# Two projections as seven block products: a hybrid streaming encoder step on one core

## The chip, the core and the metric

The kernel runs on one core of a Trainium2 chip. The metric is device time in microseconds (us) of one execution; lower is better. TensorE (PE) multiplies matrices into the eight banks of PSUM; VectorE (DVE), ScalarE (ACT) and GpSimd (POOL) do elementwise work; SyncE (SP) issues the DMA transfers between DRAM and SBUF. Before the change three runs took 1732.12, 1733.9 and 1737.66 us, median 1733.9. A difference under 0.3% (5 us) cannot be told from none.

## What is computed

One layer over 4096 prompt tokens and 32 sample tokens, width 1024, all in float32:

```
h = rmsnorm_pre(x); z = h @ w_in        # 1024 -> 2832 columns
aq 512, ak 128, av 128, ag 512, gq 256, gk 256, gv 512, gg 512, glr 16 = split(z)
attn = window_attention(rotary(aq), rotary(ak), av, sinks) * silu(ag)   # 8 heads, own chunk of 64 and the 2 before
log_a = log_sigmoid(glr @ w_gk_up + b_gk) / 16
o, state = gla_chunked(gq, gk, gv, log_a, s0)                           # 4 heads, recurrent state
o = rmsnorm(o) * silu(gg)
y = x + rmsnorm_post(concat(attn, o) @ w_out)
```

Outputs are y for prompt and sample, the last K and V rows, and the new states.

## The kernel before

**Arithmetic.** A float32 operand is split into two fp32r parts, high and low (`split` L111, `split_w` L115). A product is three matmul passes: x_high·w_high, x_high·w_low, x_low·w_high. The 32 sample tokens are stacked as high rows and low rows of one stationary tile, so that two passes do, and the two row groups are added afterwards.

**Blocks and stages.** The tokens go in 16 blocks of 256, two tiles of 128. Three stages follow one another, each over all blocks. (1) GLA: q and k are projected transposed (columns of w_in as the stationary operand, 256 tokens as the moving one: `proj_T2`, L188), then values, gates and the low-rank column group for each token tile with x as the stationary operand and 384 + 384 + 272 weight columns moving (`proj_N`, L202). A chain of small matmuls per block (decay, scores, state, output, L437 to L533) runs beside the projections of the next block; its result goes to `mixg_d` in DRAM. (2) Attention: five pairs of column tiles per block (k and v; two pairs of gates; two pairs of q), all by `proj_T2`. The chain per token tile: V transposed (L718), scores (L753), maximum, exponentials (L773), sum and scaling (L783), probabilities transposed (L800), values (L816, L824), times the gate; result to `mixa_d`. (3) Output projection: 512 + 512 columns per token tile with x as the stationary operand, then the norm and the residual (L896 to L904). Stage 2 and stage 1 both load x again from DRAM and split it (ScalarE the high part, GpSimd the low part, L112 and L113).

**Rotation.** q and k leave PSUM by ScalarE (raw, L628). VectorE shuffles (sw, L629), GpSimd multiplies by the sine rows (L630), VectorE multiplies raw by the cosine rows (L631) and adds both (L633).

**What sets the order.** TensorE's order is written out by a program. The projection of a block is a generator that yields after some matmuls and says how long these take; each chain is a generator that says after how much of that time its next step is due. A chain of block b is put into its lane when the projection of b is through, and between two parts of the projection every chain step that is due is issued. In the attention chain the wait after the scores is 9800 (in ns of such time) and after the transposes 2700. The last GLA block's chain waits 17000, so that the lane lags behind during the whole of stage 2. The order on the other engines comes from a scheduler.

**Memory.** Working tiles have rings of their own (`BUFS`, six classes); weights have slots wa, wb, wc that are loaded anew for each stage.

## Time and profile before

| | |
|---|---|
| median of three runs | 1733.9 us |
| the profiled execution | 1728.69 us, its span 1726.9 us |
| first matmul | 6.41 us |
| stages | GLA to about 690 us, attention to about 1317, output to 1718.5, then the last norm and store |
| mean granted TensorE clock | 0.992 |

The span goes from the first to the last instruction. A granted clock of 1 is 2.4 GHz, 0.5 is 1.2 GHz.

### The profile page before, as it was taken

To read this page: it belongs to the slowest core of one execution; us is meant where nothing else is said; L and a number is where in the kernel's file an instruction comes from. 1 tells how busy PE (TensorE), PEld (TensorE's weight loads), DVE (VectorE), ACT (ScalarE), POOL (GpSimd) and SP (SyncE) were. 2 spreads that over 40 slices of the span, in tenths; PEclk is the share of its full clock that TensorE was granted. 3 is DMA by queue.
4 is the path that set the end of the run, shared out by engine and by line. 5 is a ranking of instruction groups with operands and counts; after the bars stand their busy time and mean duration, and the time that the engine had idled before them with its cause. 6 is when DMAs were issued, how large, how long until landed. Compare 5 with 4: busy or idle time off the path is not lost. (4 is left out here: it accounts for less than half of the span.)

```text
span 1726.9 us, 31972 instructions
## 1 busy us (share of the span) xinstructions
PE 1680.6 (97%) x12584; PEld 1549.0 (90%) x12584; DVE 875.1 (51%) x2201; ACT 717.2 (42%) x1902; POOL 467.6 (27%) x425
## 2 busy tenths in 40 slices
PE   8899999999999999999999999999999899999998
PEld 8799999999999999999999889999998688888886
DVE  5444444454444445755555556455557633343333
ACT  7444444444444444534344344454445422222221
POOL 3222222221222222343333333333432122212220
PEclk9999999999999999999999999999999999999999
DMA  8322222221212222521111112111214444444441
GB/s 278 44 65 65 65 65 68 69 64 59 70 65 65 65 65 83 132 57 58 54 55 48 49 47 62 48 48 47 64 42 142 143 129 141 143 122 147 146 137 65
DMA packets 130855, 146.01 MB, mean 85 GB/s; under 512 B 27936, under 2 KB 103792, under 8 KB 130704
## 3 DMA queue, kind: packets, MB, share of 16 engines
q1 hardware_dynamic: 130704, 143.96, 28.1%
q8 instruction: 99, 1.62, 0.4%
q14 instruction: 52, 0.43, 0.1%
HBM read 109.67 MB, written 34.26 MB: 83 GB/s over the span
## 5 line engine op out<-in xcount | busy, mean ns | idle before, releaser
L113 POOL TENSOR_TENSOR oxl<-xst,oxh 128x512 fp32r<-128x512 f32 x64 | 82.7, 1295 | 286.1 <-DMA xo<-in_x 113.9
L773 ACT ACTIVATE pp<-pss,nb 128x192 f32<-128x192 f32 (+3 forms) x260 | 105.2, 426 | 90.1 <-DVE nb L759 66.1
L113 POOL TENSOR_TENSOR gxl<-xst,gxh 128x512 fp32r<-128x512 f32 (+1 forms) x63 | 82.2, 1307 | 167.3 <-ACT gxh L112 101.0
L896 DVE TENSOR_TENSOR yw<-pso,npw 128x512 f32<-128x512 f32 x64 | 44.2, 692 | 160.7 <-PE pso L202 160.1
L897 ACT ACTIVATE yt<-pso 128x512 f32<-128x512 f32 x64 | 38.1, 595 | 181.3 <-DVE yw L896 181.3
L424 POOL TENSOR_TENSOR xg<-xg,esg 128x512 f32<-128x512 f32 (+1 forms) x33 | 42.9, 1299 | 254.4 <-ACT esg L423 248.8
L113 POOL TENSOR_TENSOR axl<-xst,axh 128x512 fp32r<-128x512 f32 (+1 forms) x64 | 87.5, 1380 | 66.7 <-ACT axh L112 47.4
L630 POOL TENSOR_TENSOR sw<-sw,rows 128x512 f32<-128x512 f32 (+1 forms) x50 | 66.4, 1328 | 104.6 <-DVE sw L629 97.7
L672 POOL TENSOR_TENSOR sgT<-sgT,ea 128x512 f32<-128x512 f32 (+1 forms) x34 | 41.9, 1234 | 184.8 <-ACT ea L671 183.2
L783 DVE TENSOR_SCALAR pp<-pp,ll 128x192 f32<-128x192 f32 (+3 forms) x260 | 83.3, 395 | 1.1
L755 DVE TENSOR_REDUCE mx<-pss 128x2 f32<-128x384 f32 (+3 forms) x130 | 63.4, 542 | 26.9 <-PE pss L753 26.8
L202 PE MATMUL psn<-gch,gxh 128*128 128x272 f32 x256 | 73.7, 288 | 0.0
L202 PE MATMUL psn<-gcl,gxh 128*128 128x272 f32 x256 | 73.6, 287 | 0.0
L202 PE MATMUL psn<-gch,gxl 128*128 128x272 f32 x256 | 73.5, 287 | 0.0
L112 ACT ACTIVATE oxh<-xst 128x512 fp32r<-128x512 f32 x64 | 40.3, 630 | 53.2 <-DMA xst<-mixa_d 20.7
L518 ACT ACTIVATE og<-po 128x256 f32<-128x256 f32 (+1 forms) x66 | 21.7, 381 | 93.3 <-PE po L515 93.3
L485 DVE COPY_PREDICATED ats<-msk,pa 128x256 f32<-128x256 uint8 (+1 forms) x66 | 25.3, 436 | 67.1 <-PE pa L483 67.1
L112 ACT ACTIVATE axh<-xst 128x512 fp32r<-128x512 f32 (+1 forms) x64 | 40.9, 644 | 41.8 <-PE psa L188 25.8
L773 ACT ACTIVATION_READ_ACCUMULATOR pp<-pss,nb 128x1 f32 x260 | 55.9, 215 | 0.0
L633 DVE TENSOR_TENSOR q<-raw,sw 128x512 f32<-128x512 f32 (+1 forms) x34 | 39.2, 1153 | 30.3 <-POOL sw L630 30.3
L800 PE MATMUL ppT<-ident,pp 128*128 128x128 f32 (+1 forms) x388 | 49.3, 275 | 4.5 <-DVE vT L650 4.0
L804 ACT COPY pT<-ppT 128x512 f32<-128x512 f32 (+1 forms) x65 | 35.1, 585 | 44.2 <-PE ppT L800 44.1
(872 smaller groups left out, 6036.4 us busy)
## 6 DMA issues: line engine op xcount, KB each, us to landing
xst<-in_xT SPq DMA_DIRECT2D x128, 256.0 KB, 2.8
xn<-in_x SPq DMA_DIRECT2D x32, 512.0 KB, 5.2
xo<-in_x SPq DMA_DIRECT2D x64, 256.0 KB, 3.8
out_y<-yt SPq DMA_DIRECT2D x64, 256.0 KB, 2.5
wst<-in_w_in SPq DMA_DIRECT2D x32, 256.0 KB, 5.1
mixg_d<-mxg SPq DMA_DIRECT2D x16, 512.0 KB, 4.2
mixa_d<-sgT SPq DMA_DIRECT2D x16, 512.0 KB, 2.9
xst<-mixa_d SPq DMA_DIRECT2D x32, 256.0 KB, 2.7
```

The costliest lines, as they stand in the source:

```text
L112: nc.scalar.activation(hi, src, AF.Copy)
L113: (eng or nc.vector).tensor_tensor(lo, src, hi.bitcast(F32), op=ALU.subtract)
L202: nc.tensor.matmul(pss[g], a, w_of(k_, hl, g), start=(k_ == 0 and i == 0), stop=(k_ == KC - 1 and i == len(passes) - 1))
L424: nc.gpsimd.tensor_tensor(xg, xg, e, op=ALU.mult)
L630: nc.gpsimd.tensor_tensor(sw, sw, c["RS"].unsqueeze(1).to_broadcast([P, m, n]), op=ALU.mult)
L633: nc.vector.tensor_tensor(out, rv, sv, op=ALU.add)
L672: nc.gpsimd.tensor_tensor(xa, xa, e, op=ALU.mult)
L755: nc.vector.tensor_reduce(mx[:, u, g], pss[u, g][:, :, :nk], axis=AX.X, op=ALU.max)
L773: nc.scalar.activation(pps[g][b][:, u, o_ : o_ + nk], pss[u, g][:, b, :nk], AF.Exp, scale=0.125, bias=nb[:, u, g, b : b + 1], accum_out=ll ...
L783: nc.vector.tensor_scalar(pv, pv, ll[:, u, g, b : b + 1], None, op0=ALU.mult)
L800: nc.tensor.transpose(ps[:rows, g, b], src, ident)
L896: nc.vector.tensor_tensor(yw[g], pss[g][:pt], O["npw"][:pt, 512 * g : 512 * g + 512], op=ALU.mult)
```

## The change

**Products.** Two projections are computed block-wise, by the seven products of Strassen's method in Winograd's form: values/gates (2 × 260 columns for either half of the columns; 512 values or gates and 8 of the 16 low-rank columns make 520) and the output projection (2 × 512). One unit is a pair of token tiles × the two halves of K × the two halves of the columns. From the quarters A11, A12, A21, A22 of x come the sums T1 to T4, from the quarters of the weights V11, V12, V21, V22 the sums S1 to S4; seven products instead of eight are accumulated in the banks Y, X and Z, and each result is put together at the exit of a bank. Block 0 does without: it has 192 matmuls of 260 columns (output: 96 of 512) on V11, S1 = V22 + V21, V22 and V12. The sample rows take 64 (output: 32). Blocks 1 to 15 have 168 (output: 84). The weights S2, S3, S4 are made during block 0. For block b the products are issued as `stage_b` of b, `stage_a` of b+1, `stage_c` of b.

**Four stages.** (1) values/gates go to DRAM (`vl_d`, `gl_d`), silu applied to the gates; (2) q, k and the attention gates, 192 matmuls of 256 columns per block, with the GLA chain; x's split parts and the attention gates go to DRAM (`xs_d`, `sg_d`); (3) k, v, q of attention, 144 matmuls per block, with the attention chain, x read already split; (4) output. A chain may now be launched in the middle of a projection (`launch`). The attention chain waits 7400 after the scores and 100 after the transposes, and the values of a tile follow two tiles later. Half of the scaling of the probabilities moves to ScalarE.

**Slots.** Working tiles share slots with the weights (`RINGS`: per stage a list of slots in turn).

```diff
-    BUFS = {"A": (2048, 6), "B": (2048, 6), "C": (2048, 6), "D": (2048, 7), "E": (4096, 3), "F": (1024, 9)}
+    COMBOS = ("V11", "V12", "S1", "S2", "S3", "V22", "S4")
+    RINGS = {
+        "raw1": k_(*range(6)), "T1": k_(6, 7, 8, 9), "out1": k_(*range(10, 17)), "e1": k_(17, 18),
...
+        "rs": k_(0, 1, 2, 3), "rows": k_(12, 13), "kb": k_(14, 15, 18), "vT": k_(4, 5), "q": k_(*range(6, 12)),
...
+    def product(outs, name, x_, first):
+        xh, xl = x_
+        n = outs[0].shape[1]
+        for j, o_ in enumerate(outs):
+            for k in range(4):
+                wh, wl = [t_[:, j * n : j * n + n] for t_ in W[name][k]]
+                for i, (a, b) in enumerate(((xh, wh), (xh, wl), (xl, wh))):
+                    nc.tensor.matmul(o_, a[:, k], b, start=(first and k == 0 and i == 0), stop=(k == 3 and i == 2), skip_group_check=True)
+            yield 12 * n / 2.4, j
...
+    def stage_a(c, ng, n, ev):
+        c["Y"] = [mm_bank("psY")[:, :n] for _ in range(ng)]
+        for t_, j in product(c["Y"], "V11", c["A11"], True):
+            ev(c, "P1", j)
+            yield t_
+        c["X"] = [ch_bank("psX")[:, :n] for _ in range(ng)]
+        for t_, j in product(c["X"], "V12", c["A12"], True):
...
+    def stage_b(c, ng, n, ev):
+        for t_, j in product(c["Y"], "S2", c["T2"], False):
+            ev(c, "P6", j)
+            yield t_
+        c["Z"] = [ch_bank("psZ")[:, :n] for _ in range(ng)]
+        for t_, j in product(c["Z"], "S3", c["T3"], True):
+            yield t_
+        for t_, j in product(c["Y"], "S1", c["T1"], False):
...
+    def stage_c(c, ng, n, ev):
+        for t_, j in product(c["Y"], "S4", c["A22"], False):
...
+        for t_, j in product(c["Z"], "V22", c["T4"], False):
...
+        def s34(k, with_s2):
+            st, s1, v11 = s2(k)
+            if with_s2:
+                split(*w_combo("S2", k, n), st, nc.gpsimd)
+            nc.vector.scalar_tensor_tensor(s1, s1, sc(1, k), v11, op0=ALU.mult, op1=ALU.subtract)
+            s3h, s3l = w_combo("S3", k, n)
+            nc.scalar.activation(s3h, s1, AF.Copy, scale=-1.0)
+            nc.vector.scalar_tensor_tensor(s3l, s1, -1.0, s3h.bitcast(F32), op0=ALU.mult, op1=ALU.subtract)
+            v12 = ld(1, 2, k)
+            nc.vector.scalar_tensor_tensor(v12, v12, sc(2, k), st, op0=ALU.mult, op1=ALU.subtract)
+            split(*w_combo("S4", k, n), v12, nc.gpsimd)
...
-        pairs = [gs[:2], gs[2:], kvs, qs[:2], qs[2:]] if blk == 0 else [kvs, gs[:2], gs[2:], qs[:2], qs[2:]]
-        for pair in pairs:
+        for pair in (kvs, qs[:2], qs[2:]):
...
+        for c in cs:
+            launch(c["key"], attn_chain(c))
...
-                        nc.vector.tensor_scalar(pv, pv, ll[:, u, g, b : b + 1], None, op0=ALU.mult)
+                        if g == 0:
+                            nc.scalar.activation(pv, pv, AF.Copy, scale=ll[:, u, g, b : b + 1])
+                        else:
+                            nc.vector.tensor_scalar(pv, pv, ll[:, u, g, b : b + 1], None, op0=ALU.mult)
...
                 pps = scores(i)
-            if A["open"]:
-                A["open"].pop()()
-            yield 9800
+            if not smp and len(A["open"]) > 1:
+                A["open"].pop(0)()
+            yield 7400
             with tc.high_priority(PR):
                 pT = transp(i, pps)
-            A["open"].append(lambda i=i, pT=pT: finish(i, pT))
-            yield 2700
...
+                A["open"].append(lambda i=i, pT=pT: finish(i, pT))
+            yield 100
...
+    for ld, pj, pj_s in ((load1, proj1, proj1_s), (load2, proj2, None), (load3, proj3, None), (load4, proj4, proj4_s)):
+        for b in range(NBLK):
+            phases.append((ld, pj, b))
```

TensorE in the attention stage, before: psa is a projection (aa5 a gate weight), pvt V transposed, pss the scores, poT the values.

```order
5685 L188 MATMUL psa<-axl,aa5h 128x256
5686 L188 MATMUL psa<-axh,aa5l 128x256
5687 L718 MATMUL pvt<-ident,vT 128x128 [waits DVE_49]
5688 L718 MATMUL pvt<-ident,vT 128x128
5689 L753 MATMUL pss<-kb,q 128x192 x8
5690 L816 MATMUL poT<-pT,v 64x128 [waits Activation_49]
```

TensorE at the border of two blocks in stage 3 now: aq7 is the last weight of the pair q2, q3, ppT the transposed probabilities.

```order
7489 L313 MATMUL psa<-axl,aq7h 128x256
7490 L313 MATMUL psa<-axh,aq7l 128x256
7491 L1015 MATMUL ppT<-ident,pp 128x128 [waits Activation_49] x2
7492 L1015 MATMUL ppT<-ident,pp 128x128 [waits DVE_49] x2
...
7498 L1015 MATMUL ppT<-ident,pp 128x128 x3
7499 L930 MATMUL pvt<-ident,vT 128x128 [waits Activation_49]
7500 L930 MATMUL pvt<-ident,vT 128x128
7501 L965 MATMUL pss<-kb,q 128x192 [waits DVE_49]
7502 L965 MATMUL pss<-kb,q 128x192
7503 L965 MATMUL pss<-kb,q 128x192 [waits DVE_49]
7504 L965 MATMUL pss<-kb,q 128x192 x5
```

The scores of a tile stood in the middle of a gate projection and waited for nothing new; now they stand behind the last projection of q and wait for VectorE twice, for q0, q1 and for q2, q3.

VectorE at the same border now: sw, raw and q are the rotation of q2, q3, mx the maximum of the scores.

```order
1126 L1017 COPY pT<-ppT 128x512 [waits PE_49]
1127 L844 STREAM_SHUFFLE sw<-raw 128x512 [waits Activation_49]
1128 L846 TENSOR_TENSOR raw<-raw,rows 128x512 [waits DVE_49]
1129 L848 TENSOR_TENSOR q<-raw,sw 128x2x4x64 [waits DVE_49,Pool_49]
1130 L967 TENSOR_REDUCE mx<-pss 128x2 [waits PE_49] x4
```

The copy of the transposed probabilities stands ahead of the rotation, and the maxima right behind it.

VectorE near the start, before (qf and kf leave block 0's banks, psb, behind the last weight splits):

```order
49 L117 SCALAR_TENSOR_TENSOR gb7l<-wst,npre_sb,gb7h 128x256 [waits DMAHW2_49,Activation_49]
50 L117 SCALAR_TENSOR_TENSOR gcl_197<-wst,npre_sb,gch_195 128x256 [waits Activation_49]
51 L375 SCALAR_TENSOR_TENSOR qf<-psb,Rp 128x512 [waits DMAHW2_49,PE_49]
52 L375 SCALAR_TENSOR_TENSOR kf<-psb,Rp 128x512 [waits PE_49]
```

And now (c_701, c_697 and c_710 are exits of block 0's banks ps; wst are weights that S2, S3 and S4 are made of):

```order
73 L278 TENSOR_TENSOR wst<-wst 128x520 [waits DVE_49]
74 L288 SCALAR_TENSOR_TENSOR wst<-wst,npre_sb 128x520
75 L455 TENSOR_SCALAR c_701<-ps_379,rs 128x260 [waits DVE_49,PE_49]
76 L291 SCALAR_TENSOR_TENSOR S_2l<-wst,S_2h 128x520 [waits Activation_49]
77 L275 TENSOR_SCALAR wst<-wst,npre_sb 128x520 [waits DMAHW7_49,Pool_49]
78 L455 TENSOR_SCALAR c_697<-ps_378,rs 128x260 [waits DVE_49]
```

The exits of block 0 stand between the operations that make S3 and S4, with more of 520 columns ahead of them than there were splits before.

## Rows read from the trace of the kernel before

**Rows 1.** The page: busy time, share of the span, instructions of each engine.

```profile
PE 1680.6 (97%) x12584; PEld 1549.0 (90%) x12584; DVE 875.1 (51%) x2201; ACT 717.2 (42%) x1902; POOL 467.6 (27%) x425
```

**Rows 2.** By stretch: length, busy time (instructions) per engine, granted clock, DMA share, GB/s.

```profile
0.00:40.00 40.00, 33.59 (x227) 33.30 (x227) 24.27 (x54) 29.86 (x62) 11.72 (x19) 1.00 0.88 279
40.00:65.00 25.00, 17.29 (x115) 16.42 (x115) 8.65 (x18) 12.31 (x25) 9.79 (x8) 0.86 0.60 92
...
690.00:890.00 200.00, 197.50 (x1808) 188.51 (x1808) 121.89 (x295) 92.60 (x259) 77.13 (x66) 1.00 0.26 71
890.00:1090.00 200.00, 190.62 (x1754) 181.69 (x1753) 117.41 (x296) 86.26 (x286) 69.82 (x73) 0.97 0.17 50
```

**Rows 3.** Timeline of TensorE, 256 columns, dense: start us, duration us.

```profile
842.72 0.28 PE L188 MATMUL psa<-axh,ab6h 128*128 128x256 f32 x1
...
845.07 0.28 PE L188 MATMUL psa<-axh,ab1l 128*128 128x256 f32 x1
```

**Rows 4.** Timeline of TensorE in values/gates, one pass of a k step apart.

```profile
200.32 0.29 PE L202 MATMUL psn<-gcl,gxh 128*128 128x272 f32 x1
...
200.79 0.29 PE L202 MATMUL psn<-gch,gxl 128*128 128x272 f32 x1
```

**Rows 5.** Timeline of TensorE in the output projection, 24 matmuls apart.

```profile
1499.62 0.39 PE L202 MATMUL pso<-oa0h,oxh 128*128 128x512 f32 x1
...
1505.20 0.39 PE L202 MATMUL pso<-ob0h,oxh 128*128 128x512 f32 x1
```

**Rows 6.** A group of VectorE: busy us, mean ns, idle before, its releaser.

```profile
L117 DVE SCALAR_TENSOR_TENSOR ga0l<-wst,npre_sb,ga0h 128x512 fp32r<-128x512 f32 x1 | 0.8, 752 | 1.3 <-ACT ga0h L116 1.3
```

**Rows 7.** By stretch, at the start, columns as in rows 2.

```profile
10.00:20.00 10.00, 10.00 (x87) 10.00 (x87) 7.91 (x21) 9.27 (x23) 3.33 (x2) 1.00 1.07 376
20.00:30.00 10.00, 10.00 (x65) 10.00 (x64) 8.97 (x19) 9.87 (x22) 2.51 (x1) 1.00 0.93 312
```

**Rows 8.** TensorE's waits: us in total, times, longest.

```profile
PE ppT L800 <- DVE vT L650: 4.0, 2, 2.6
...
PE pvt L718 <- DVE pT L802: 1.7, 1, 1.7
```

**Rows 9.** Timeline of a rotation of q and the transposes beside it.

```profile
843.98 0.59 ACT L628 COPY raw<-psa 128x512 f32<-128x512 f32 x1 [1.65 <-PE psa L188]
...
844.61 0.75 DVE L629 STREAM_SHUFFLE sw<-raw 128x512 f32<-128x512 f32 x1
...
845.20 1.48 PE L800 MATMUL ppT<-ident,pp 128*128 128x128 f32 x12
845.39 0.69 DVE L631 TENSOR_TENSOR raw<-raw,rows 128x512 f32<-128x512 f32 x1
...
845.43 1.81 POOL L630 TENSOR_TENSOR sw<-sw,rows 128x512 f32<-128x512 f32 x1 [1.73 <-DVE sw L629]
846.00 0.68 DVE L802 COPY pT<-ppT 128x512 f32<-128x512 f32 x1
...
846.42 0.36 PE L188 MATMUL psa<-axh,ab2h 128*128 128x256 f32 x1
...
847.19 1.30 POOL L113 TENSOR_TENSOR axl<-xst,axh 128x512 fp32r<-128x512 f32 x1
...
847.27 1.76 DVE L633 TENSOR_TENSOR q<-raw,sw 128x512 f32<-128x512 f32 x1 [0.59 <-POOL sw L630]
...
849.39 1.57 PE L753 MATMUL pss<-kb,q 64*128 64x192 f32 x16
```

**Rows 10.** A group of VectorE, columns as in rows 6.

```profile
L633 DVE TENSOR_TENSOR q<-raw,sw 128x512 f32<-128x512 f32 x30 | 35.9, 1195 | 30.3 <-POOL sw L630 30.3
```

**Rows 11.** Timeline of TensorE: the end of a gap, in brackets.

```profile
906.61 0.44 PE L718 MATMUL pvt<-ident,vT 128*128 128x128 f32 x2 [1.67 <-DVE pT L802]
```

**Rows 12.** By stretch, behind that gap, columns as in rows 2.

```profile
907.60:910.00 2.40, 2.40 (x28) 1.87 (x24) 1.75 (x4) 1.64 (x3) 0.62 (x1) 0.52 0.00 0
910.00:913.00 3.00, 3.00 (x35) 2.59 (x28) 1.64 (x5) 2.24 (x12) 0.65 (x1) 0.82 0.00 0
```

1061 lines of the change are left out of this document (621 added, 440 removed).

## The prediction

> **What bounds the kernel now.** I read the busy shares first. TensorE is busy 97% of the span and no other engine over 51% [rows 1], so a column of matmul saved is time saved, unless the new order makes TensorE stand. The table by stretch says where it already stands: 40 − 33.6 and 25 − 17.3 us at the start (14.1 us together), then 2.5 and 9.4 in two stretches of 200 us of the attention stage [rows 2]. So the prediction is two sums: what the seven products save, and what TensorE stands more or less than before.
>
> The price of a matmul is the distance from start to start in a dense run, not its duration. With 256 columns, 20 steps take 2.35 us, 117.5 ns each [rows 3]. One token tile's k step of a pass in values/gates, 384 + 384 + 272 columns, takes 0.47 to 0.48 us; I use 0.475 [rows 4]. With 512 columns, 24 steps take 5.58 us, 232.5 ns [rows 5]. Between 256 and 512 a column costs 0.45 ns, so 260 columns are estimated at 119.3 ns; it is interpolated between rows that lie close.
>
> **The products.** Before, values/gates are 32 tiles × 8 k × 3 passes, and 16 steps of the sample: 784 triples × 0.475 = 372.4 us. After, block 0 has 192 matmuls of 260 columns (no products), the sample 64, and blocks 1 to 15 have 7 products × 24 = 168 each: 2776 × 0.1193 = 331.2 us, −41. The output projection was 1568 × 0.2325 = 364.6 us; it becomes 96 + 32 + 15 × 84 = 1388, 322.7 us, −42. Other matmuls keep their number. **Sum: −83 us.** Moving the attention gates and qk into stage 2 changes no matmul. The sums of inputs (four subtractions per block pair of tiles on VectorE, seven splits on ScalarE and GpSimd) and the exits of the products lie beside about 20 us of products a block (168 × 0.1193, 84 × 0.2325). ScalarE is the fullest, with some 25 operations of about 0.6 us (raw, a copy of 512 columns, took 0.59 [rows 9]) a block in stage 1, an estimate of 15 us; so I cost them at nothing, with rival C if that is wrong.
>
> **The start: +15 us (+2 to +25).** In the new order VectorE has 59 operations of 512 or 520 columns up to the last low half of S3 and a few small ones, before the first product of block 1 may begin (the rows of the order show the end of it). At 0.75 us each, a weight split undisturbed [rows 6], they are 44 us; five of 260 columns add some 2, and 25 tiny ones at about 0.2 another 5: 51 us. In the same phase before, VectorE was busy 7.9 and 9.0 of 10 us [rows 7]; at that 84% the 51 us become 61, from 5.5 on: product S2 of block 1 at about 67 us. Until then TensorE has 192 + 64 + 48 (V11 and V12 of block 1) matmuls, 36 us. It stands 67 − 36 = 31 us against 14, and some of the work runs at the lower clock in both. The lower bound is 51 us without any wait, the upper takes the stretching of VectorE's operations beside GpSimd. TensorE's gap comes in the middle: the sample needs the banks of block 0, whose exits stand behind the weights on VectorE and ScalarE.
>
> **The attention stage: +45 us (0 to +75).** This is the step that decides. Before, a block has five pairs of column tiles (kv, two of gates, two of q), and the chain of the block starts a whole stretch later, so the scores never wait for the rotated q: no such row is among TensorE's waits; what waits there is V or the transposed probabilities, 4.0 and 1.7 us in all [rows 8]. After, gates are gone, the chain is launched as soon as q2, q3 are projected and TensorE's order at each block's border is: last projection of q2, q3; 12 transposes of the tile before; 2 transposes of V; the scores, whose third matmul needs q2, q3 rotated. Counted from the last projection, VectorE first copies pT (its order puts the copy ahead), which starts when the first transposes are done, at 0.8 (845.20 to 846.00), and takes 0.68; then the shuffle 0.75, GpSimd's product 1.81 and the sum [rows 9]. With a sum of 0.7 to 1.2 and a tenth for handoffs q is there after 4.8 to 5.3 us; in the trace the whole chain from ScalarE's copy to the sum, with the copy of pT in it, is 843.98 to 849.03, 5.05 us [rows 9]. TensorE has 12 transposes (845.20 to 846.42, 1.2 us), two more (0.3 by the same pace and the change of shape) and two scores (1.57/16 × 2 = 0.2) to do: 1.7 to 1.8 us. The gap is 3.0 to 3.5 us; I take 3.0.
>
> A gap costs more than itself. After the 1.67 us gap before 906.61 [rows 11] the granted clock was 0.52 in the 2.4 us from 907.6 on and 0.82 in the next 3.0 [rows 12]: the lower level, 1.2 GHz, then back to 2.4. That loses 2.4 × 0.48 + 3.0 × 0.18 = 1.7 us. I assume it behind two gaps in three, 1.1 us each. Per block 4.1, 16 blocks: +66. What goes: the attention stage's own standing, 11.9 us, and its low clock, 0.97 of 200 [rows 2], 6 us: −18. Fewer changes between projection and chain: −3. The lower end is a gap that vanishes (−18, +16 for leftovers), the upper a gap of 4 us with the low clock each time.
>
> Here a rule of the Trainium skill is weighed. The sum q<-raw,sw takes 1195 ns in the mean [rows 10], and 1.76 us in the row at 847.27, while GpSimd splits x beside it (1.30 us from 847.19 on); the product raw<-raw,rows, of the same shape, took 0.69 [rows 9]. In the new stage 3, x comes already split, so GpSimd has no split there. The Trainium skill ("GPSIMD Engine Reference", Key points) says that GpSimd shares its SBUF interfaces with VectorE and contends with VectorE instructions that have two SBUF inputs. The trace agrees as far as these two rows go; by the rule the sum is 0.7 us, the gap 3.0, without it 1.2 and 3.5, 8 us more over 16 blocks.
>
> **Transitions: +7 us (0 to +15).** Before, weights change twice; after, three times, through rings of few slots that also feed the working tiles. The nearest row is the stretch at 690 us with 2.5 us lost [rows 2]. Stage 2 has the same chain beside more projection than it needs, as before. The tail is the same kind of chain after the last matmul: 0.
>
> **Sum:** −83 + 15 + 45 + 7 = −16 us, against the profiled execution's 1728.7 us: 1712.7. The median of the runs shown is 5 us above that execution, so 1712.7 to 1718; **I say 1716 us.**
>
> **Rivals.**
> A. The border hides. The scheduler's order holds, but the rotation is quicker than I think or the scores' banks and transposes take longer, so the gap is about 1 us and the clock stays up: 16 − 18 in the attention stage instead of +45, and 10 at the start, 5 at transitions: −83 − 2 + 15 = −70, 1660 us. For it: copy, shuffle, a product and a sum at their shortest (0.59, 0.75, 1.30 as GpSimd's split takes, 0.69) are 3.3 us, 1.6 more than the cover [rows 9]. Against it: that leaves out the copy of pT that the order puts ahead.
> B. The border costs more, and the change is slower. Place: the wait of the scores for q2, q3. If GpSimd's product and VectorE's sum both stretch as in the rows at 845.43 and 847.27 (1.81 and 1.76), q is there after 5.9 us, the gap is 4 us and the lower clock follows every time: 16 × (4 + 1.7) = 91 − 18 = +73; −83 + 73 + 15 + 7 = +12, so 1741, or 1746 with the 5 us to the median. It decides from 4.9 us of loss per block on: 16 × 4.9 − 18 = 61 = 83 − 22.
> C. The products do not get their pace. Their banks leave slowly, or loads come late through the shared slots, and a block of stages 1 and 4 loses 2 us: 30 × 2 = 60, so −16 + 60 = +44, 1773 us. Against it: 20 us of products stand over ScalarE's 15, and before, the same exits hid beside the same TensorE.
>
> The Trainium skill ("TensorE: Matmul & The Clock Gate", What's actually happening) says that the throttled clock is the default and activity releases it. The 0.52 after 1.67 us [rows 11, 12] agrees. If every gap of 3 us paid the 1.7 us, it would be 16 × 0.6 = 10 us above my two in three, within the range.
>
> **How the numbers follow.** Forecast 0.50 (1698 to 1734), A 0.22, B 0.18, C 0.10. The range 1670 to 1748 leaves out C and the better half of A. A difference under 0.3% (5 us) can't be told from none. Faster: most of the forecast's case (0.42) and A (0.22), 0.64. Same: 0.05 of the forecast's and 0.07 of B's and C's, 0.12. Slower: the rest, 0.24.
>
> **What would show it.** In the attention stage of the new profile, a row "scores wait for VectorE q" of about 48 us in some 16 times, 3 us each, and granted clock near 0.95. If it is under 16 us, A holds; over 60, B. In stages 1 and 4 TensorE busy throughout with steps of 119 and 233 ns; a step above 125 ns or idle TensorE there is C. At the start the product S2 of block 1 near 67 us; before 55 or after 80 the count of VectorE's queue is wrong.

## The result and the profile after

The changed kernel takes 1847.9 us in the median (1844.8 to 1855.9, 4 runs), the kernel before beside it 1733.1: ratio 1.066, interval 1.062 to 1.071. It is slower by 115 us, where 1716 us and a range up to 1748 were forecast. The profiled execution is the slowest of the four, 8 us above the median; its span is 1853.0 us against 1726.9.

First the busy times of the changed kernel, against [rows 1]:

```profile
PE 1666.7 (90%) x12828; PEld 1524.4 (82%) x12828; DVE 1054.9 (57%) x2272; ACT 861.7 (47%) x2244; POOL 715.1 (39%) x665
```

TensorE stands 1853.0 − 1666.7 = 186 us, before 46: +140. Its busy time fell by only 14, because more of it now runs at the lower clock. I add up the busy time in the stretches in which the records grant 1.2 GHz and count half of it as lost: 64.4 us, before 9.9. So 140 + 54.5 us came on, and 68.4 went from the busy time that is left: +126, the difference of the spans.

The places, in windows of the changed kernel (columns as in rows 2): the start, values and gates, stage 2 (GLA), stage 3 (attention), the beginning of the output projection and its middle.

```profile
40.00:100.00 60.00, 26.17 (x200) 25.34 (x198) 36.25 (x57) 28.32 (x60) 28.79 (x28) 0.76 0.85 184
200.00:300.00 100.00, 100.00 (x838) 100.00 (x837) 45.03 (x76) 62.99 (x131) 61.65 (x46) 1.00 0.63 140
500.00:600.00 100.00, 96.33 (x842) 90.14 (x841) 54.60 (x129) 42.41 (x97) 37.39 (x40) 1.00 0.52 166
1100.00:1200.00 100.00, 92.84 (x859) 86.42 (x858) 52.33 (x145) 44.49 (x164) 20.14 (x22) 0.95 0.36 112
1500.00:1600.00 100.00, 79.45 (x327) 60.90 (x326) 63.10 (x117) 34.67 (x77) 35.69 (x27) 0.86 0.44 136
1600.00:1700.00 100.00, 99.13 (x428) 80.01 (x427) 76.18 (x134) 45.77 (x109) 46.85 (x35) 1.00 0.48 151
```

Where the products run (200 to 300, 1600 to 1700) TensorE hardly stands at all. It stands at the start, in small holes in stages 2 and 3, and where the output projection begins. My sums of the gaps between TensorE's records and of what the lower clock costs, stage by stage ("before" is the stage that does the same work):

| stretch of the changed kernel | standing | lost to the clock | before, both | more | forecast |
|---|---|---|---|---|---|
| start, 0 to 115 us | 51.7 | 4.9 | 17.0 | 39.6 | 15 |
| values/gates and the change to stage 2, to 455 | 13.2 | 2.7 | 1.9, with stage 2 | 14.0 | part of 7 |
| stage 2, to 960 | 23.3 | 13.0 | (in the row above) | 36.3 | 0 |
| stage 3, to 1455 | 53.1 | 27.8 | 16.7 | 64.2 | 45 |
| output, its beginning to 1590 | 30.7 | 13.9 | 20.9, with the rest | 23.7 | part of 7 |
| output, the rest | 14.6 | 3.1 | (in the row above) | 17.7 | 0 |

Together 195 us, of which 67 were forecast. The first row is somewhat high: in nine later runs whose start is the same, standing up to 115 us is 42.7 to 48.3 us, and with the clock they come to 34 to 38 us more than before.

What TensorE waited for (columns as in rows 8):

```profile
PE pss L965 <- DVE q L848: 45.0, 17, 4.7
PE pss L248 <- DVE c L455: 26.4, 1, 26.4
PE po L675 <- DVE Sn L669: 13.0, 11, 2.1
PE poT L1031 <- ACT pp L985: 11.0, 4, 8.0
PE psu L592 <- ACT qk3h L148: 9.2, 1, 9.2
PE psY L169 <- ACT c L1135: 8.0, 4, 3.8
PE pgl L584 <- POOL gl L567: 7.5, 3, 4.9
```

L965 are the attention's scores, L248 the sample's rows at the start, L675 the outputs of GLA, L592 and L584 the first decays of stage 2, L1135 the exits in the output projection. The forecast named the places of the first two, the start's as the sample behind block 0's exits; the others it did not have.

The pace of the products, from the timeline of TensorE: 24 matmuls of 260 columns, then 8 of 512.

```profile
249.82 0.28 PE L169 MATMUL psX<-V_0h,A12h 128*128 128x260 f32 x1
...
252.69 0.28 PE L169 MATMUL psY<-S_0h,A22h 128*128 128x260 f32 x1
...
1650.97 0.39 PE L169 MATMUL psY<-S_0h,T1h 128*128 128x512 f32 x1
...
1652.82 0.40 PE L169 MATMUL psY<-S_2h,T1l 128*128 128x512 f32 x1
```

2.87/24 = 119.6 ns and 1.85/8 = 231 ns, where 119.3 and 232.5 were reckoned.

One border of stage 3, timeline of all engines, against [rows 9]:

```profile
1120.76 1.47 PE L1015 MATMUL ppT<-ident,pp 128*128 128x128 f32 x12
1121.40 0.69 DVE L1017 COPY pT<-ppT 128x512 f32<-128x512 f32 x1 [0.99 <-PE ppT L1015]
...
1122.02 0.72 DVE L844 STREAM_SHUFFLE sw<-raw 128x512 f32<-128x512 f32 x1
1122.07 0.38 PE L930 MATMUL pvt<-ident,vT 128*128 128x128 f32 x2
1122.38 0.59 PE L965 MATMUL pss<-kb,q 64*128 64x192 f32 x4
...
1122.89 1.70 POOL L845 TENSOR_TENSOR sw<-sw,rows 128x512 f32<-128x512 f32 x1 [3.20 <-DVE sw L844]
...
1124.62 0.69 DVE L848 TENSOR_TENSOR q<-raw,sw 128x512 f32<-128x512 f32 x1 [1.15 <-POOL sw L845]
...
1125.37 2.07 PE L965 MATMUL pss<-kb,q 64*128 64x192 f32 x12 [2.39 <-DVE q L848]
```

It is the forecast's chain: copy of pT, shuffle, GpSimd's product, sum, then the scores that need q. The sum takes 0.69 us here and 721 ns in the mean of 30, where it took 1195 before [rows 10]; GpSimd has no split beside it now. The Trainium skill ("GPSIMD Engine Reference", Key points) has VectorE's instructions with two SBUF inputs contend with GpSimd; this sum agrees with it. So q came after 4.55 us (4.8 to 5.3 were forecast), TensorE had 2.2 us of work to cover it (1.7 to 1.8 were), and the gap is 2.39 us instead of 3.0.

Behind it the granted clock, in two windows, against [rows 12]:

```profile
1125.00:1128.00 3.00, 2.63 (x24) 2.20 (x28) 1.88 (x5) 0.00 (x0) 0.79 (x2) 0.61 0.53 170
1128.00:1131.00 3.00, 3.00 (x38) 2.50 (x31) 1.66 (x6) 2.22 (x12) 0.62 (x1) 0.82 0.03 8
```

The clock fell after this gap. Between the first and the last projection of the stage the scores waited 16 times for q, and 15 of these gaps had a stretch at the lower clock at them or within 6 us behind; the one at 1290 had none. 25.3 us were lost there, 1.6 for each gap: nearly the 1.7 of rows 12 every time, not in two gaps of three.

### The profile page after: what moved, and what is told of

Read it like the earlier page. It is cut to its first block, busy times and chain, and to the rows that moved or that the text cites. A ratio compares the mean times of both kernels' runs of the same rounds, so it can differ in the third digit from the quotient of the medians.

```text
span 1853.0 us, 34426 instructions
## 1 busy us (share of the span) xinstructions
PE 1666.7 (90%) x12828; PEld 1524.4 (82%) x12828; DVE 1054.9 (57%) x2272; ACT 861.7 (47%) x2244; POOL 715.1 (39%) x665
## 4 chain that ended last, share of the span: by engine, by line
PE 55%; DVE 10%; DMA 4%; issue 2%; ACT 2%; POOL 2%; SPq 0%; DVEq 0%; POOLq 0%; ACTq 0%
PE psb L313 15%; PE psa L313 12%; PE psY L169 7%; PE psZ L169 3%; PE pss L965 2%; DMA wst<-in_w_out 2%; PE poT L1039 2%; PE psX L169 2%; POOL sw L845 1%; PE ppT L1015 1%; PE psb L303 1%; PE poT L1031 1%; PE psa L303 1%; PE pa L646 1%; PE ps L169 1%
## 5 line engine op out<-in xcount | busy, mean ns | idle before, releaser
L985 ACT ACTIVATE pp<-pss,nb 128x192 f32<-128x192 f32 (+2 forms) x260 | 105.3, 427 | 116.4 <-DVE nb L971 78.5
L145 POOL TENSOR_TENSOR gxl<-xst,gxh 128x512 fp32r<-128x512 f32 x68 | 85.1, 1258 | 145.3 <-ACT gxh L144 126.5
L965 PE MATMUL pss<-kb,q 64*128 64x192 f32 (+3 forms) x520 | 65.1, 385 | 46.1 <-DVE q L848 45.0
L965 PEld LDWEIGHTS pss<-kb,q 64*128 64x128 f32 x520 | 48.0, 211 | 57.0 <-DVE q L848 50.4
L313 PE MATMUL psa<-axh,kv 128*128 128x256 f32 x480 | 94.1, 294 | 0.0
L205 DVE TENSOR_TENSOR T<-xq 128x512 f32<-128x512 f32 x60 | 64.9, 1082 | 45.9 <-POOL T3l L145 31.5
L313 PEld LDWEIGHTS psa<-axh,kv 128*128 128x128 f32 x480 | 79.1, 199 | 2.8 <-issue 2.4
L205 DVE TENSOR_TENSOR T<-xq,T 128x512 f32<-128x512 f32 x60 | 62.2, 1037 | 17.8 <-POOL T4l L145 12.9
L313 PE MATMUL psa<-axl,kv 128*128 128x256 f32 x240 | 69.9, 291 | 0.0
L145 POOL TENSOR_TENSOR T3l<-T,T3h 128x512 fp32r<-128x512 f32 x30 | 42.8, 1425 | 56.4 <-DVE w_x L140 27.8
L145 POOL TENSOR_TENSOR T4l<-T,T4h 128x512 fp32r<-128x512 f32 x30 | 39.4, 1313 | 61.0 <-ACT T4h L144 51.9
L145 POOL TENSOR_TENSOR A22l<-xq,A22h 128x512 fp32r<-128x512 f32 x32 | 45.8, 1431 | 35.5 <-ACT A22h L144 32.4
L145 POOL TENSOR_TENSOR A12l<-xq,A12h 128x512 fp32r<-128x512 f32 x32 | 43.3, 1352 | 35.1 <-ACT A12h L144 35.1
L145 POOL TENSOR_TENSOR T2l<-T,T2h 128x512 fp32r<-128x512 f32 x30 | 39.2, 1308 | 45.0 <-ACT T2h L144 34.7
L1019 ACT COPY pT<-ppT 128x512 f32<-128x512 f32 (+1 forms) x65 | 35.1, 587 | 42.7 <-PE ppT L1015 42.5
```

The costliest lines, as they stand in the source:

```text
L145: (eng or nc.vector).tensor_tensor(lo, src, hi.bitcast(F32), op=ALU.subtract)
L205: sub = lambda a, b, nm: (lambda t_: (nc.vector.tensor_tensor(t_, a, b, op=ALU.subtract), t_)[1])(sl(ring, [P, 4, P], nm))
L313: nc.tensor.matmul(ps[:, j], a, b[:, :TB], start=(k == 0 and j == 0 and i == 0), stop=(k == KC - 1 and j == 1 and i == 2))
L965: nc.tensor.matmul(pss[u, g][:, b, :nk], c["q"][b][r_, 2 * i + u].rearrange("p j t -> p (j t)"), kb[r_, k0 : k0 + nk], start=True, stop=True)
L985: nc.scalar.activation(pps[g][b][:, u, o_ : o_ + nk], pss[u, g][:, b, :nk], AF.Exp, scale=0.125, bias=nb[:, u, g, b : b + 1], accum_out=ll ...
L1019: nc.scalar.copy(pT[:rows], ps[:rows])
```

## The experiments

Every ratio is to the kernel before in the same runs; the changed kernel stands at 1.066, and 0.01 is 17 us. "Up to 115 us" and the like are my sums as in the table.

### Stage 3: the border

**e1_lag.** The attention chain of block 0 starts 6 us of planned work later; since the chains of the blocks run one behind the other, all do.

```
+        if blk == 0:
+            yield 6000
         vtransp()
...
-            yield 100
+            yield 280
```

> The attention chain of the first block starts 6 us of projection later, and its last wait is 280 instead of 100, so that the chain keeps this lag: a block's scores now stand some 6 us behind the last projection of q, everything else as in the changed kernel (1847.9 us). Theory (the border of the blocks costs its wait for the rotated q and a low clock behind it): the scores' wait for VectorE's q, 45.0 us in 17 times, falls under 6 us, the time lost to the low clock in stage 3 falls from 27.8 to under 10 us, and the whole from 1848 to about 1785 (1778 to 1800). Rival (the order of the border is not what counts; the waits only move to the next step, probabilities or banks): the q wait goes, but waits of the transposes and values take its place, 25 us or more of them, and the time stays above 1820.

Measured 1.034 (1.032 to 1.037), 55 us less. The waits of TensorE that are left:

```profile
PE pss L248 <- DVE c L455: 23.3, 1, 23.3
...
PE ppT L1015 <- ACT pp L996: 11.0, 8, 3.9
PE poT L1031 <- ACT pp L985: 10.5, 4, 5.3
...
PE pss L965 <- DVE q L848: 4.3, 1, 4.3
```

The scores' wait for q, 45.0 us, has sunk to 4.3; the transposes now wait 11.0 us for the probabilities (L996). From the first to the last projection of stage 3, standing falls from 45.9 to 20.2 us and what the clock costs from 25.3 to 8.3, 43 us together. Behind that, in the output projection, the two fall by another 14 us; why they do is not shown. The theory holds: the border was the largest single term, and it is one of order, not of work.

### Stage 2: the outputs of GLA

The row to be explained is po (L675), waiting 13.0 us in 11 times. The low clock came at its two longest waits, 2.1 us each. Three attempts failed before one held.

**e3_decay_banks.** The decay's two banks come from the projection's ring, so that it takes none from the ring of po.

```
-        pt_ = ch_bank("pgl")
+        pt_ = mm_bank("pgl")
...
-        pu = ch_bank("psu")...
+        pu = mm_bank("psu")...
```

> In stage 2 the two banks of the decay chain are taken from the projection's ring of four PSUM banks instead of the chain's ring; nothing else differs from the changed kernel (1847.9 us). Theory (the decay of the next block and the chain of this block now run interleaved in one ring of four banks, and po gets the bank that pu has just left to VectorE): po's wait for VectorE's Sn, 13.0 us in 11 times, falls under 4 us, the clock loss of stage 2 (13 us) falls by half, gain 12 to 22 us: about 1831. Rival (VectorE is simply behind in stage 2, so the wait comes back at another step of the chain): the sum of TensorE's waits in stage 2 stays within 5 us of 25, gain under 5 us.

1.065 (1.063 to 1.067): nothing gained, po's wait 13.1 us. The rival holds.

**e5_mix_gap.** The pieces of the mix are spaced otherwise: the yields 2500, 3000, 2600, 3400 become 2200, 2500, 2200, 4600.

```
-        yield 3400
+        yield 4600
```

> In stage 2 the chain's waits are 2200, 2500, 2200 and 4600 instead of 2500, 3000, 2600 and 3400, so that 4600 instead of 3400 of projection lie between the outputs of a block's two tiles; the rest is the changed kernel (1847.9 us, 1.066 times the kernel before). Theory (the second tile's po needs a bank that VectorE's Sn leaves, and VectorE, which now has the decay of the next block in the same stretch, gets there about 1.1 us too late): po's wait, 13.0 us in 11 times, falls under 4 us, and the clock loss of stage 2, 13 us, to 5; gain 12 to 18 us, ratio about 1.057. Rival (the wait is VectorE's load and comes back at the first tile or at the scores): gain under 4 us, ratio 1.064 or more.

1.079 (1.075 to 1.083), slower. po now waits for og and for the gate's exponentials:

```profile
PE po L675 <- DVE og L687: 10.0, 5, 2.9
...
PE po L675 <- ACT ea L322: 8.4, 5, 1.7
```

**e10_po_banks.** po's two banks come from the projection's ring.

```
-            po = [ch_bank("po")...
+            po = [mm_bank("po")...
```

> In stage 2 the two banks of po of each tile are taken from the projection's ring of four instead of the chain's ring; the rest is the changed kernel (ratio 1.066). Theory (po waits for a bank: four chain banks for pa, pk, pu, po, px and the decay, where po is held until VectorE has the row factors): po's waits, 14 us in 12 times, fall under 4 us, gain 12 to 20 us with the clock, ratio 1.055 to 1.059. Rival (no bank but VectorE's and ScalarE's pace; the projection then waits for banks instead): TensorE's waits in stage 2 stay above 20 us, ratio 1.063 or more.

1.093 (1.091 to 1.095): much slower, po waits 18.0 us for og and 16.5 for the gates (ea), which I take to be the projection's banks coming free behind them (not shown). More room in the chain's ring (e3) does not help, and taking from the projection's ring hurts.

What then showed it was the order of VectorE beside one such wait in the changed kernel:

```profile
575.22 1.21 DVE L601 TENSOR_TENSOR_SCAN ta<-rst,tb 128x512 f32<-128x512 bf16 x1
...
576.24 0.66 PE L667 MATMUL pu<-vf,kn 128*64 128x128 f32 x8
576.40 0.68 DVE L747 TENSOR_TENSOR sgT<-psb,Rp 128x512 f32<-128x512 f32 x1
576.83 0.71 PE L675 MATMUL po<-vf,ats 128*128 128x128 f32 x4
577.00 0.68 DVE L604 COPY cm<-ta 128x4 f32<-128x4 f32 x1
577.72 0.43 DVE L605 TENSOR_TENSOR ta<-ta,cm 128x256 f32<-128x256 f32 x1
578.13 0.42 DVE L669 TENSOR_TENSOR Sn<-pu,Sm 128x256 f32<-128x256 f32 x1
578.61 0.71 PE L675 MATMUL po<-vf,ats 128*128 128x128 f32 x4 [1.06 <-DVE Sn L669]
```

The second half of po waits for the sum L669. Its input pu is there at 576.9, but in VectorE's order the next block's decay (the scan L601, L604, L605), the exit of an attention gate (L747) and the norm of the tile before stand ahead of it, and it starts at 578.13. In the kernel before, the scan mostly started some 16 us ahead of the next such sum; now it is some 3 us.

**e13_decay_later.** The decay begins 2.5 us of planned work later.

```
-    def decay(c, wait=12500):
+    def decay(c, wait=15000):
```

> One number: the next block's decay chain begins 15000 instead of 12500 ns of planned work behind the block's start in stage 2. Theory (in stage 2 the sum that frees the bank of po stands on VectorE behind the next block's scan, L601, and its copy and subtraction, L604 and L605): the scan then falls behind that sum; po<-Sn goes from 13.0 us to under 4, stage 2 (455 to 960) from 23.3 us idle and 13.0 lost to the low clock to about 14 and 7, the time falls by some 15 us: ratio near 1.058. Rival (VectorE is late with whatever stands there, not with the scan): another release takes its place (og, or the decay's own tiles at the next block's q and k), the time within 5 us of the changed kernel's, 1.063 to 1.070, or above.

1.055 (1.053 to 1.057), 20 us less. The waits in stage 2, and the window that stood at 96.33:

```profile
PE px L697 <- DVE og L687: 4.9, 3, 4.2
...
PE po L675 <- DVE tb L595: 1.5, 2, 0.8
PE po L675 <- DVE Sn L669: 0.9, 2, 0.7
...
500.00:600.00 100.00, 100.00 (x869) 94.47 (x868) 57.29 (x138) 41.28 (x98) 39.14 (x44) 1.00 0.53 167
```

From the first projection of stage 2 to the first of stage 3, standing is 15.3 us (was 35.2) and the loss to the clock 3.4 (was 15.7). The theory holds: in most blocks the scan now starts some 20 us ahead of the next such sum. The gain in the ratio, 20 us, is a little over the 15 expected; that of the two profiled executions is larger, and one of them is the slowest of its four runs.

**e14_no_scan.** The scan and the subtraction behind it are left out of the 16 blocks.

```
-            nc.vector.tensor_tensor_scan(ta..., G["rst"], tb..., ...)
-            nc.vector.tensor_copy(cmv, tav[:, :, 0, 63])
-            nc.vector.tensor_tensor(tav[:, :, 0, :], ..., op=ALU.subtract)
+            nc.vector.tensor_copy(cmv, tb[:, 0, 0:4])
```

> Leaves out the scan of the decay and the subtraction behind it in the 16 blocks of stage 2 (L601 and L605; L604 copies other numbers in their place): 1.21 + 0.43 us of VectorE a block. Theory (that piece of VectorE's order makes po late): po<-Sn under 4 us, stage 2 idle near 12, the time down by 15 to 20 us, ratio 1.055 to 1.058. Rival (the late thing is the chain of the mix itself, one tile's state behind the other's): po<-Sn stays at 9 us or more and the time within 5 us.

1.060 (1.057 to 1.063), 11 us less, po waits 7.7 us: between the two. Taking two of the pieces away helps half as much as moving the whole chain out of the way, so these two are only a part of what stood ahead of the sum. Neither the theory (under 4 us) nor its rival (9 us or more) came.

**e8_lag_gap_f4.** e1's lag, e5's spacing, and the first decay 4 us later (edits as in e1 and e5; `decay(cs[0], 0)` becomes `decay(cs[0], 4000)`).

> Three edits at once: the lag of the attention chain (measured: ratio 1.034), the wider gap between the outputs in stage 2, and the first block's decay in stage 2 due 4 us of projection later, so that TensorE does gate projections while the constants of the decay come (a wait of 8.5 us and low clock behind it). Theory: they add up: −54, −12 to −18 and −8 to −11 us, ratio 1.018 to 1.026. Rival (the gaps of stage 2 come back elsewhere): ratio 1.030 or more. No theory expects it to beat the kernel before.

1.052 (1.050 to 1.055), worse than the lag alone by 31 us. The first decays wait less (psu 4.1 us, not 9.2), but e5's spacing costs here too (po waits 8.4 us for ea and 8.4 for og), and the exits in the output projection wait 17.2 us (psY for c).

**e16_lag_decay.** e1's and e13's edits together.

> The lag of the attention chain (ratio 1.0343 alone) with the decay's later begin. The two stand in different stages. Theory: the gain of the later decay adds, ratio near 1.026. Rival: the later decay gives nothing, ratio 1.031 to 1.038.

1.026 (1.022 to 1.030): the two gains add, 0.040 together where they were 0.032 and 0.012 alone.

### The start

TensorE stands 26.4 us before the sample's rows, up to 71.1 us. The engines in that hole, from the timeline of the changed kernel:

```profile
60.58 0.76 DVE L276 SCALAR_TENSOR_TENSOR wst<-wst,npre_sb 128x520 f32<-128x520 f32 x1
...
65.79 1.06 ACT L336 ACTIVATE xn<-xn 128x1024 f32<-128x1024 f32 x1 [5.00 <-DMA xn<-in_x]
...
68.59 0.49 DVE L277 TENSOR_SCALAR wst<-wst,npre_sb 128x520 f32<-128x520 f32 x1 [7.25 <-DMA wst<-in_w_in]
...
70.59 0.49 DVE L455 TENSOR_SCALAR c<-ps,rs 128x260 f32<-128x260 f32 x1
...
71.14 0.58 PE L248 MATMUL pss<-V_0h,stk 128*128 128x260 f32 x1 [26.39 <-DVE c L455]
```

VectorE isn't full: it stands 7.25 us at a weight that hasn't landed. The exit of block 0 (L455), which would free TensorE, stands behind the sums on that weight. ScalarE stands in the same way at the loads of x for the row norms.

The experiments on the start are read by TensorE's standing up to 115 us and by when stage 2 begins, against the nine runs with the start unchanged (42.7 to 48.3 us; stage 2 from 389.7 to 396.9) and the changed kernel (51.7; 395.0).

**e2_late_sums, e6_sums_behind_sample.** The sums for S2 to S4 are issued behind the exits of block 0 (e2), and behind those of the sample (e6).

```
-                todo, after = [...], 2
+                todo, after = [...], 100
...
-            if (pj, b) == (proj1, 0):
+            if pj is proj1_s:
```

(the first line for both, the second for e6 alone)

> In stage 1 the sums of weights S2, S3, S4 are issued behind the exits of block 0 instead of between them; nothing else differs from the changed kernel (1847.9 us). Theory (placement: in-order VectorE and ScalarE hold block 0's exits, and with them the banks that the sample needs, behind weight sums that wait for their DMA): TensorE's 26.4 us wait falls under 8 us, part of it comes back in front of the first product of block 1, and the kernel gains 12 to 20 us: about 1832. Rival (throughput: the first product of block 1 needs all of S2 and S3, and these come when DMA and VectorE are through with them, wherever they stand): the wait only moves behind the sample, the gain is under 5 us.

> In stage 1 the weight sums S2, S3, S4 are issued behind the exits of the sample rows, so that no exit of block 0 or of the sample stands behind them; the rest is the changed kernel. When they stood between the two, the wait only moved. Theory (throughput: loads, VectorE and GpSimd need some 50 us for the sums, and the first product of block 1 needs them all): S2's first product comes no earlier than 85 us (88.9 now), TensorE stands about as long as now in one piece behind V11 and V12 of block 1, ratio 1.062 to 1.075. Rival (placement after all: the sums behind all exits are done as fast as before and the exits hide): S2's first product at 70 to 78 us, gain 10 to 18 us, ratio about 1.057.

e2: 1.072 (1.069 to 1.074); the 26.4 us are gone, and 34.6 us stand before the first product of block 1 in their place, for the sample's exits; S2 starts at 104.7 us, not 88.9. e6: 1.086 (1.084 to 1.089); 16.4 us stand before the first product of block 1, for the sample's exits; S2 starts at 88.8, but its parts come one by one (waits of 10.4, 16.5 and 6.2 us). The wait only moved.

**e7_no_sums1.** The sums for S2 to S4 of stage 1 are left out.

```
-                todo, after = [lambda k=k: V1["s34"](k, True) for k in range(4)], 2
+                todo, after = [... for k in range(0)], 2
+                W.update(S2=W["V11"], S3=W["V12"], S4=W["V22"])
```

> In stage 1 the weight sums S2, S3, S4 are left out (16 loads, 28 operations of VectorE, the splits), and products use V11, V12, V22 in their place; the row scale is an eighth, so that the numbers stay in range. The outputs are not the reference's. It prices the sums: theory, with the sums gone block 1's products start right behind V11 and V12, at about 50 to 56 us instead of 88.9; the waits of 26.4 and 6.8 us and the low clock behind them go: gain 33 to 42 us, ratio about 1.044. Rival (the start is held by the loads of x, the row norms and the gates' exits as much as by the sums): gain under 18 us, ratio above 1.056.

1.074 (1.073 to 1.076): no gain, but this number is spoilt by the edit. The first line below is at the start, the second in stage 4:

```profile
PE psY L169 <- DVE zs L254: 17.4, 1, 17.4
PE pss L248 <- ACT S_1h L290: 13.4, 1, 13.4
```

After the edit `W["S2"]` is the same list as `W["V11"]`, and so for the other two pairs. When stage 4 enters its own S2, S3 and S4 in these lists, it overwrites V11, V12 and V22, and its sample rows then read the sums and wait for them, some 29 us in four waits. In the 100 us behind stage 3's last projection TensorE stands 48.9 us, where it stands 32.0 in the changed kernel. e15 and e17 have the same edit.

The start itself is not touched by that. Standing up to 115 us is 42.0 us and stage 2 begins at 393.6, so leaving out the sums alone still gives nothing there. The first product of block 1 stands 17.4 us for the sample's exits. These stand behind ScalarE's squares, which wait for their loads, and GpSimd stands 10.7 us at a small product that waits for the row scale Ra (more on it at e15).

**e9_third_slot, e12_lag_slot.** The row norms' tiles of x take three slots instead of two from block 2 on; e12 has e1's lag besides.

```
-            xn = el_tile(V1["nx"] % 2, [P, D], "xn")
+            xn = el_tile(V1["nx"] % 2 if V1["nx"] < 6 else (V1["nx"] + 2) % 3, [P, D], "xn")
```

> In stage 1 the tiles of x whose squares ScalarE sums for the row norms take turns in three slots instead of two, from the first tile of block 2 on; that one goes into the slot of the sample's stacked rows, so it can't be loaded before the sample's matmuls. On ScalarE the squares of blocks 2 to 5 then stand behind the exits of block 0 and of the sample; before they stood between them. The rest is the changed kernel (ratio 1.066). Theory (the start is held by ScalarE, in order behind squares that wait 5 to 10 us for their load): the wait of 26.4 us falls under 14 and the 6.8 under 3, S2's first product comes at 70 to 76 us instead of 88.9, gain 12 to 20 us, ratio 1.055 to 1.059. Rival (the loads and sums for S2 to S4 set the start): S2's first product at 85 or later, gain under 5 us, ratio above 1.063.

> The lag of the attention chain (alone 1.034) and the third slot of the squares together. The two places are 900 us apart, so they should add up: with the theory of the start 1.023 to 1.027, with its rival 1.031 to 1.036. Neither expects it under 1.02, since stage 2 (about 35 us of waits and low clock) and the start of stage 4 (about 40) are as they were.

1.072 (1.070 to 1.073) and 1.043 (1.041 to 1.045). e9 can't be told from the changed kernel; e12 is worse than e1 by 15 us. The wait before the sample stays at 23.8 and 23.5 us, and a new one comes at 121 and 125 us, 8.8 and 12.1 long, for an exit of ScalarE (psY for c).

**e11_no_norm_loads.** The loads of x for the row norms are left out; the first tile is squared each time.

```
+            if "xn" not in V1:
+                V1["xn"] = [el_tile(j, [P, D], f"xn{j}") for j in range(2)]
+                nc.sync.dma_start(V1["xn"][0], x[0:P])
-            nc.sync.dma_start(xn[:pt], x[t0 + i * P : t0 + i * P + pt])
```

> In stage 1 the loads of x for the row norms are left out (33 loads, up to 512 KB each): all squares are taken of the first tile of x, so the norms and with them the outputs are not the reference's; each square is done as before. Theory (ScalarE waits for these loads, with the exits of block 0 and of the sample behind it): ScalarE has no wait for x in the first 100 us, TensorE's waits of 26.4 and 6.8 us fall to under 14 together, gain 15 to 25 us with the clock, ratio 1.052 to 1.058. Rival (the sums' loads and VectorE hold the start): gain under 6 us.

1.066 (1.065 to 1.068): no gain. Standing up to 115 us is 46.5 us, and the wait before the sample is 27.8.

**e15_start_bare.** Both leave-outs of e7 and e11 together (edits as there).

> Leaves out both things that the start has beside block 0's own work: the sums for S2, S3 and S4 of stage 1 (V11, V12 and V22 stand in their place) and the row norms' loads of x (the first tile is squared each time). Each alone left the time where it was or above. Theory (the two queues, DMA with ScalarE's squares and DMA with VectorE's sums, are late together, and either alone holds the start): idle time of TensorE up to 115 us falls from 51.7 to near 22 us, S2's first product stands near 66 us, the time falls by 25 to 32 us, ratio 1.048 to 1.052. Rival (a third thing holds it: the weights V12 and V22 with S1, or the exits of block 0 and the sample): idle stays above 38 us, the time within 10 us of the changed kernel's.

1.068 (1.066 to 1.070), spoilt in stage 4 as e7 is (48.1 us behind stage 3's last projection). At the start standing up to 115 us falls to 33.4 and stage 2 begins at 375.1, 15 us earlier than in the earliest run with the old start. That standing lies between the theory's 22 us and the rival's 38. The window that was to be full isn't:

```profile
40.00:60.00 20.00, 12.40 (x104) 12.19 (x103) 2.89 (x7) 8.95 (x21) 3.04 (x5) 0.86 0.15 17
...
56.96 0.25 POOL L835 TENSOR_TENSOR RC<-RC,Ra 128x32 f32<-128x32 f32 x1 [22.19 <-DMA Ra<-rs_d]
...
57.38 1.26 POOL L145 TENSOR_TENSOR T3l<-T,T3h 128x512 fp32r<-128x512 f32 x1
```

From 40 to 60 us no engine is full. GpSimd stands 22.2 us at two small products that belong to the sample in **stage 3**: their tiles have no one to wait for, so the scheduler put them here, and the row scale Ra that they need has to come back from DRAM. The splits of block 1 (L145) stand behind it, VectorE's subtractions and the exits behind those.

**e17_bare_late_rows.** As e15, and Ra takes its slot in the ring of the other row scales, so that the two products stand in stage 3.

```
-                c["R"], c["RC"], c["RS"] = [small(nm, NS)[:, :n] for nm in ("Ra", "RC", "RS")]
+                c["R"] = sp.tile([P, TB], F32, name="Ra", tag="Rp", bufs=2)[:, :n]
+                c["RC"], c["RS"] = [small(nm, NS)[:, :n] for nm in ("RC", "RS")]
```

> Leaves out the same two things as e15_start_bare (the sums for S2 to S4 of stage 1, the row norms' loads of x) and puts one more: the row scale of the sample in stage 3 takes a slot of the ring of the other row scales, so that GpSimd's product with it stands in stage 3 and not in the first 60 us. In e15_start_bare GpSimd stood 22.2 us at that product, waiting for the row scale to come back from DRAM, and TensorE 18.1 us behind it. Theory (that wait is the third thing): TensorE's wait psY<-zs goes from 18.1 us to under 6, idle time up to 115 us from 33.4 to near 20, the time falls by 12 to 16 us against e15_start_bare: ratio 1.058 to 1.061. Rival (the exits' own chain through the sample's row norm holds it): the wait stays above 12 us, the ratio above 1.064.

1.061 (1.058 to 1.065). The waits at the start are now few:

```profile
PE ps L448 <- ACT V_0h L148: 6.8, 1, 6.8
PE psY L169 <- DVE zs L254: 4.0, 1, 4.0
```

Standing up to 115 us is 19.0 us, and the product that takes S2's place (that of T2) starts at 65.2: nearly the 14.1 of before. So three things hold the start together: the sums with their loads, the norms' loads, and a product of stage 3 that came too early. The sums or the norms' loads alone, taken away, leave the others: GpSimd stands at the early product 0.4 us in the changed kernel, 10.7 without the sums (e7), 5.5 without the norms' loads (e11) and 22.2 without both. Moving the early product with only one of the two left out was not tried.

The time follows only in part. Stage 2 begins 32.5 us earlier than in the changed kernel, but the program as a whole gains 9 us by the ratios (21 by the two profiled executions). The 100 us behind stage 3's last projection stand 46.4 us instead of 32.0, by the shared lists of e7; without that the gain would be some 23 us, an estimate from these two numbers.

**e18_lag_decay_rows.** e16 with Ra's slot as in e17, nothing left out.

> e16_lag_decay (ratio 1.0261) with the sample's row scale of stage 3 in the ring of the other row scales, nothing left out. Theory (in the full kernel three queues hold the start together; GpSimd waited only 0.4 us at that product in the changed kernel): no gain over 3 us, ratio 1.022 to 1.030. Rival (the product holds VectorE's and ScalarE's order behind GpSimd in the full kernel too): pss<-c falls from 23.9 us to under 15 and the ratio to 1.02 or under.

1.025 (1.021 to 1.029). In the full kernel the early product costs little, as GpSimd waits there only 0.4 us for Ra; the wait before the sample goes from 23.9 to 20.8 us, where runs with the same start have 21.3 to 26.4. It is not told from e16. This is the best version that I ran, and it is slower than the kernel before.

### The beginning of the output projection

**e4_no_sums4.** The sums for S3 and S4 of the output's weights are left out.

```
-                for k in range(4):
-                    s34_4(k, False)
+                W.update(S3=W["V12"], S4=W["V11"])
```

> In stage 4 the weight sums S3 and S4 are left out: their 16 loads, 28 operations of VectorE and the splits are gone, and the products use V12 and V11 in their place, so the output rows of blocks 1 to 15 are not the reference's. Theory (the sums can only start when the attention chain has left their slots, near 1496 us, and the products of block 1 wait for them): TensorE's waits between 1505 and 1590 (about 21 us) and the low clock behind them (about 9 us) go, gain 25 to 32 us: about 1820. Rival (the start of stage 4 is held by other things: the attention chain's end, the posts of block 0 and of the sample, loads of x): gain under 12 us.

1.053 (1.051 to 1.055), 23.5 us less. The window that stood at 79.45 with clock 0.86:

```profile
1500.00:1600.00 100.00, 96.25 (x405) 77.46 (x404) 61.59 (x118) 43.48 (x101) 45.18 (x33) 0.97 0.41 128
```

The tiles of these sums take the slots of stage 3's probabilities, transposes and V, and its last values end at 1501.9 us. In the changed kernel the loads are issued from 1506.8 on, into slots that the residual's tiles use as well, and the last S_3 is there at 1544.2, while S3's products would be due. Which of the two sets of slots holds the sums back wasn't tested; that the sums hold the products, e4 shows.

## Why the prediction was wrong, step by step

- **Products, −83:** right in pace (119.6 and 231 ns) and in sum. If each matmul is charged the time to the next one's start or to its own end, and the lower clock is taken out, values/gates and the output projection fall from 384.9 + 365.9 to 337.1 + 324.6 us, −89. The other matmuls keep their number and take 20 us more, so that TensorE's busy time net of the clock fell by only 68.4; why they take more stays open. Rival C did not come: in values/gates TensorE is busy 100 of 100 us.
- **Border, +66:** the mechanism is right, and the wait is 45.0 us in 17 times against 48 in 16. The term that was too low is the clock behind it, assumed after two gaps in three (17.6 us): it fell behind nearly every one, and the stage lost 27.8. Other waits of the stage made 8 us more, where 0 was put in. What went is 16.7 us, close to the −18. So 45.0 + 27.8 + 8.1 − 16.7 = +64. That is near rival B's +73, though the sign named for B (over 60 us of waiting) did not come and the forecast's did. e1 takes the wait away and gains 55 us; by the two profiled executions 43 of them lie in this stage.
- **Start, +15:** the step that failed is "at that 84% the 51 us become 61": it took VectorE's load for the bound. Place and count were right: the sample waits for block 0's exits, and 59 operations of 512 and 520 columns stand up to S3's last low half. But these took 53.8 us, not 44, VectorE stood 10.3 us at weights that had not landed, and the last was done at 81.4 us, not 67. In-order queues were late one behind another: the weights for the sums, ScalarE's squares at the loads of x, the exits of block 0 and of the sample behind both. The start came to +39.6 (34 to 38 in the other runs). e2 and e6 show that moving the sums does not help, e7 and e11 that neither the sums nor the norms' loads hold it alone, e15 and e17 that both do together, and then the early product.
- **Stage 2, at nothing:** "the same chain beside more projection than it needs, as before" looked at whether there was work to hide the chain, not at the order on VectorE. The chain of one block and the decay of the next are now closer together, 3 us instead of 16, and a sum on which TensorE waits fell behind a scan on which nobody waits yet. That is +36 by the table, 20 us of it shown by e13.
- **Transitions, +7:** mis-sized. The change to stage 2 stands 9.2 and 7.5 us at the decays of the first blocks, and the beginning of the output projection stands for sums of weights; e4 gives 23.5 us for these alone. "Rings of few slots that also feed the working tiles" was written down and then priced by a row of a kernel whose working tiles shared no slots with the weights.
- **The clock:** 54.5 us more in all, against some 18 that were put in. I priced it at the border alone. In stage 2 seven holes of 1.06 to 1.61 us had no lower clock behind them, but five of 2.05 to 4.9 us had it at them or just behind; the long waits at the start and at the output's beginning had it too.

So what doesn't show in instruction counts was 195 us against the 67 forecast, and the saving of the products was there. No version of the order that I ran brings the kernel under the time of before: with the border and stage 2 mended, 44 us remain to be found at the start, at the transitions and in the output's beginning.

## What to carry to other kernels

When a change cuts the bound engine's work but also reorders the rest, price every border where one stage's tiles become another's slots, from what must be finished before the first load may even be issued. On an engine that runs in order, ask of each small operation that the bound engine needs what stands just ahead of it; moving something nobody yet waits for by 2.5 us gave back 20 us here. If taking one cause away does nothing, take two away together before giving the theory up. And look through the whole trace of a kernel with a part left out: here the leave-out of e7 cost 17 us more standing 1400 us further on, by two names for one list.

## What the runs showed of the hardware

- Behind gaps of mostly 2.4 us in stage 3 the granted clock was at the lower level for a stretch in 15 cases of 16, 1.6 us lost for each, so that such a gap costs some 4.0 us. With most of these gaps gone (e1) the loss fell from 25.3 to 8.3 us. The seven holes of 1.06 to 1.61 us of stage 2 were followed by no such stretch.
- A subtraction of two SBUF tiles of 512 columns at the start (L205, in e15_start_bare) took 1.73 us at 58.67, with a split of GpSimd beside it from 58.60 to 59.86, and 0.69 us at 62.87, with GpSimd standing; the first ended 0.54 us behind the split. The Trainium skill ("GPSIMD Engine Reference", Key points) names that contention; here it is a factor of 2.5, in the stretch that had least to spare.
